# A hybrid decoder layer on one core: outputs stored as high and low parts, the state update added up in PSUM, a one-column mix on ScalarE, and other figures in the kernel's order model

## The chip, the core and the metric

The program runs on one core of one Trainium2 chip. The metric is the device time of one execution in microseconds (us). TensorE (PE in the profile) multiplies; its weight loads are PEld. VectorE is DVE, ScalarE is ACT, GpSimd is POOL, and SyncE (SP) issues nearly all DMAs.

## What is computed

One layer over 2048 tokens of width 1024, all in float32. Cut to what matters here:

```python
h = LN(x) * (1 + scale) + shift
proj = h @ w_in                                  # 1024 x 4232
rw = rw + (rw_prev - rw) * rwkv_mix              # mix with the token before
# group A, RWKV-7, 8 heads x 64, for each token:
S = S * w_t - (S @ kk_t) b_t^T + v_t k_t^T       # S is 64 x 64 per head
y_a = S @ r_t
# group B, 8 heads x 64: causal softmax attention with a running forget bias
y = concat(GN(y_a) + bonus, y_b) * silu(gate)
out = LN(alpha * x + (1 + gate_c) * (y @ w_out))
```

## The kernel before, in words

**Projections.** TensorE multiplies float32 by splitting each operand into a high part (rounded to fp32r) and the rest: three fp32r matmuls of 128 x 512 per 128-row slice, 24 for a tile of 128 columns and 512 tokens. The weight tile is loaded into `wst` (one buffer), copied to the high part in `wsp` by ACT, and POOL subtracts to get the low part (`weights()`; `wsp` has two buffers, `wb`). There are 66 weight tiles of the input projection with 48 matmuls each, and 16 token tiles of the output projection, also with 48, for which the stored outputs `yscr` take the place of the weights.

**Stages.** The 2048 tokens go in two halves of 1024. For each half the recurrence (`rwkv_stream`, tiles named `rw_s`) comes first and then attention (`fox_stream`, tiles `fx_s`, `fx_p`, `fx_v`). Projection matmuls (`ps<-ht,wsp`) are put between the small matmuls of these stages as filler. Output tiles of the first half serve as filler in the second attention stage; the others follow it, half of all with the tiles `end_s`.

**The recurrence.** It works on chunks of 64 tokens. A batch (`rwkv_batch`, 64 of them: two halves, 8 blocks, 4 batches) does two chunks for a pair of heads. X (`xs`) holds solved right sides for keys and values; Z holds score and key matrices. Before, four matmuls of 128 x 128 x 128 in plain float32 make F = X^T Z for keys and values together; DVE adds two matrices to the key half with four instructions, and ACT copies the value half with two. The state tile then holds [S; I] per head (the unit matrix in the other half of its rows), so that one matmul of 128 rows gives the key part times S plus the value part. Per chunk four matmuls follow, two that give the next state and two that give y, and DVE scales the two halves of the state with two instructions. A plain float32 matmul leaves two records in the trace, an fp32r one or a transpose one.

**The finish.** `rwkv_post` and `fox_out` multiply a result of 128 x 512 by its gate and store it (32 stores). `final_x` reads x again for a token tile and normalises it with DVE, POOL, DVE. `final_tile` runs 48 matmuls; `final_evac` adds on DVE, takes mean and variance, and applies four `scalar_tensor_tensor` of 128 x 512 before the stores.

**What sets the order.** The instructions are not scheduled by the compiler: the kernel's `Driver` runs all streams as generators against its own table of costs (`cost`, `on_pe`) and issues next whatever its clock says is ready, by priority. So each engine's queue is fixed when the program is built, and each engine runs its queue strictly in order. A figure in that table changes the order everywhere behind it. `drv.side()` marks work whose end the stream does not wait for.

`hs(h)` picks rows 0 to 63 or 64 to 127, so that the matmuls of two heads use different parts of the array.

Of the kernel before, what the change touches and what calls it, by code (L numbers as in the profile page):

```python
# [17 lines left out]
D = 1024  # L18
TB = 1024
NB = 512  # L20
# [117 lines left out]
class Driver:  # L138
# [31 lines left out]
    def cost(self, e, op, ops, kw):  # L170
# [3 lines left out]
        if "dma_start" in op:  # L174
            return 450.0 if e.name == "sp" else 1000.0
# [35 lines left out]
    def on_pe(self, t, op, ops):  # L211
# [6 lines left out]
        if nr == nc == 4:  # L218
            d = max(stream + (14 if n >= 256 else 3), load + 2)
        else:  # L220
            d = max(stream + (load if nc < 4 else 6), 25.0)
# [113 lines left out]
def hymba_kernel(ctx: ExitStack, tc, x, c, emb_ln_g, emb_ln_b, w_ada, b_ada, w_in, rwkv_mix, w0,  # L335
# [47 lines left out]
    yscr = [dram.tile([D, TB], F32, name=f"yscr{i}") for i in range(2)]  # L383
# [35 lines left out]
    state = const.tile([128, 2, 4, 2, 64], F32, name="state")  # L419
# [156 lines left out]
    def start_consts():  # L576
# [82 lines left out]
        for b in range(2):  # L659
            for p in range(4):  # L660
                dve.tensor_copy(state[64:128, b, p, 0, :], i64[64:128, :])
                dve.tensor_copy(state[0:64, b, p, 1, :], i64[0:64, :])
            yield
# [200 lines left out]
    def weights():  # L864
# [4 lines left out]
        while True:  # L869
# [77 lines left out]
    def shift_mix(b, g, o):  # L947
# [5 lines left out]
        dve.scalar_tensor_tensor(o[:, 0:1], car[:, g:g + 1], par("mix", g), o[:, 0:1],  # L953
                                 op0=OP.mult, op1=OP.add)
# [452 lines left out]
    def rwkv_batch(p, n, c0, bufs, u, qt, yb, dl, st):  # L1407
# [6 lines left out]
        Xh = xs.ap.rearrange("p (i c) -> p i c", c=128)  # L1414
# [17 lines left out]
        bf = b.ap.rearrange("p (i c) -> p i c", c=128)  # L1432
        for h in range(2):
            i = slice(2 * h, 2 * h + 2)
            tt(Fh[hs(h), i, 0:64], bf[hs(h), i, 0:64], kr[hs(h), g, 1], OP.add)
            tt(Fh[hs(h), i, 64:128], bf[hs(h), i, 64:128], i64[hs(h), None, :].to_broadcast([64, 2, 64]), OP.add)
        for h in range(2):
            o = hs(1 - h)
            i = slice(2 * h, 2 * h + 2)
            act.activation(Fh[o, i, :], bf[o, i, :], AF.Copy)  # L1440
# [4 lines left out]
        for ci in range(2):  # L1445
# [4 lines left out]
            for h in range(2):  # L1450
                i = 2 * h + ci
                mm(b.ap[hs(h), 0:64], Fh[:, i, 64:128], cur[:, h, :])
            with drv.side():
                for h in range(2):
                    i = 2 * h + ci
                    mm(yb.ap[hs(h), cc * 64:(cc + 1) * 64], cur[:, h, :], Fh[:, i, 0:64])
# [6 lines left out]
        st["next"] = (n, c0 + 2) if c0 + 2 < 8 else (n + 1, 0)  # L1463

    def rwkv_post(half, p, blk, yb, bonus):
# [29 lines left out]
        g.free()  # L1495
        yield
        sp.dma_start(yscr[half][p * 128:(p + 1) * 128, blk * NB:(blk + 1) * NB], Y.ap)
        Y.free()
        yield
# [35 lines left out]
    def rwkv_stream(half):  # L1535
# [20 lines left out]
        def elems():  # L1556
            for n in range(8):
# [8 lines left out]
                u.amuse = 2  # L1566
                u.done = done
# [285 lines left out]
    def fox_out(half, p, h, qi, nk, pv, o, sums):  # L1853
# [43 lines left out]
        g.free()  # L1897
        yield
        sp.dma_start(yscr[half][512 + p * 128:640 + p * 128, qi * NB:(qi + 1) * NB], o.ap)
        o.free()  # L1900
        normed[0] += 1
        yield
# [71 lines left out]
    def final_x(i):  # L1974
# [13 lines left out]
        yield  # L1988
        tt(xt.ap, xt.ap, fin["eb"].ap, OP.add)
# [115 lines left out]
```

## Time and profile before

| | us |
|---|---|
| median of 3 runs | 1866.49 |
| lowest and highest | 1865.16, 1883.88 |
| the profiled execution's own time | 1866.47 |
| its span, first to last instruction | 1864.7 |
| PE busy | 1784.5 (96%) |
| DVE busy | 1287.4 (69%) |
| ACT, POOL busy | 804.4, 779.3 |

A row of the timeline is: start us, duration us, engine, source line, operation, output tile <- input tiles, shape, xcount, and in brackets the idle time before it and what ended it. All work is issued through one helper, so every row has line L134; the tile names tell the parts apart. For matmuls the shape is rows*columns of the array, then the moving operand. Ends of matmuls are modelled, so rates are read from start to start.

### The profile page before, as it was taken

To read this page: it belongs to the slowest core of one execution; us is meant where nothing else is said; L and a number is where in the kernel's file an instruction comes from. 1 tells how busy PE (TensorE), PEld (TensorE's weight loads), DVE (VectorE), ACT (ScalarE), POOL (GpSimd) and SP (SyncE) were. 2 spreads that over 40 slices of the span, in tenths; PEclk is the share of its full clock that TensorE was granted. 3 is DMA by queue.
4 is the path that set the end of the run, shared out by engine and by line. 5 is a ranking of instruction groups with operands and counts; after the bars stand their busy time and mean duration, and the time that the engine had idled before them with its cause. 6 is when DMAs were issued, how large, how long until landed. Compare 5 with 4: busy or idle time off the path is not lost.

```text
span 1864.7 us, 35565 instructions
## 1 busy us (share of the span) xinstructions
PE 1784.5 (96%) x13609; PEld 1288.3 (69%) x13609; DVE 1287.4 (69%) x3049; ACT 804.4 (43%) x1571; POOL 779.3 (42%) x773
## 2 busy tenths in 40 slices
PE   8999999999999899999999999989899899999995
PEld 6777777767777656677777777767555356666884
DVE  4987685665773768667657675762677584876998
ACT  2454555354444245554554554443244344432000
POOL 1333242422423357743143442424256364566652
PEclk8999999998999999999999999999899899999998
DMA  8252020210122755132021120213422732512433
GB/s 263 72 163 81 30 69 23 80 51 26 53 87 86 226 172 178 58 115 84 19 78 36 41 79 30 75 39 114 131 92 84 244 111 77 191 57 90 153 115 122
DMA packets 172129, 181.60 MB, mean 97 GB/s; under 512 B 12180, under 2 KB 116197, under 8 KB 171960
## 3 DMA queue, kind: packets, MB, share of 16 engines
q1 hardware_dynamic: 171960, 179.33, 30.6%
q8 instruction: 108, 1.77, 0.4%
q14 instruction: 61, 0.50, 0.1%
HBM read 132.10 MB, written 47.13 MB: 96 GB/s over the span
## 4 chain that ended last, share of the span: by engine, by line
PE 55%; DVE 5%; ACT 3%; SPq 3%; DMA 2%; issue 2%; POOL 1%; DVEq 0%; ACTq 0%; POOLq 0%
PE ps L134 55%; SPq L134 3%; ACT rw_s L134 2%; DVE rw_s L134 2%; DMA arena<-vscr 1%; DVE end_s L134 1%; DVE small L134 1%; DVE arena L134 1%; POOL rw_s L134 0%; POOL wsp L134 0%; DMA arena<-in_b_ada_dram 0%; ACT arena L134 0%; DMA yscr<-rw_s 0%; DVE fx_p L134 0%; DMA fx_s<-qscr 0%
## 5 line engine op out<-in xcount | busy, mean ns | idle before, releaser
L134 PE MATMUL ps<-ht,wsp 128*128 128x512 f32 x3840 | 976.4, 400 | 3.4 <-POOL wsp L134 1.3
L134 PEld LDWEIGHTS ps<-ht,wsp 128*128 128x128 f32 x3840 | 701.1, 189 | 163.3 <-issue 15.0
L134 POOL TENSOR_TENSOR wsp<-wst,wsp 128x1024 fp32r<-128x1024 f32 x79 | 192.8, 2440 | 320.2 <-ACT wsp L134 256.2
L134 ACT ACTIVATE rw_s<-ps 64x256 f32<-64x256 f32 (+3 forms) x544 | 215.9, 409 | 200.7 <-PE ps L134 101.0
L134 PE MATMUL ps<-fx_s 67*128 67x512 f32 (+6 forms) x960 | 261.1, 390 | 12.3 <-DMA fx_s<-kscr 4.0
L134 ACT ACTIVATE fx_p<-ps 128x512 f32<-128x512 f32 (+3 forms) x336 | 162.8, 521 | 196.2 <-PE ps L134 175.6
L134 PEld LDWEIGHTS ps<-fx_s 67*128 67x128 f32 (+1 forms) x960 | 165.4, 193 | 118.3 <-issue 47.7
L134 POOL TENSOR_TENSOR fx_p<-fx_p 128x512 f32<-128x512 f32 (+2 forms) x160 | 185.7, 1167 | 140.7 <-PE ps L134 138.3
L134 PE MATMUL ps<-rw_s 32*32 32x32 f32 (+4 forms) x5376 | 227.7, 217 | 17.0 <-DVE rw_s L134 8.0
L134 PEld LDWEIGHTS ps<-rw_s 32*32 32x32 f32 (+3 forms) x5376 | 195.7, 130 | 66.1 <-issue 26.6
L134 DVE TENSOR_TENSOR rw_s<-rw_s 128x24 f32<-128x24 f32 (+11 forms) x544 | 179.8, 336 | 26.0 <-ACT rw_s L134 12.6
L134 DVE TENSOR_REDUCE small<-ps 128x1 f32<-128x512 f32 (+1 forms) x208 | 134.5, 683 | 44.4 <-PE ps L134 43.6
L134 ACT ACTIVATE arena<-ps 128x512 f32<-128x512 f32 (+3 forms) x128 | 74.1, 581 | 191.6 <-PE ps L134 161.7
L134 POOL TENSOR_TENSOR small<-small,nhalf 128x8 f32<-128x8 f32 (+1 forms) x48 | 68.3, 1425 | 211.6 <-DVE small L134 211.5
L134 PE MATMUL ps<-fx_p,fx_v 128*64 128x512 f32 (+3 forms) x640 | 155.9, 556 | 0.0
L134 DVE TENSOR_TENSOR fx_p<-fx_p 128x512 f32<-128x512 f32 (+1 forms) x128 | 111.9, 874 | 51.6 <-POOL fx_p L134 48.9
L134 ACT ACTIVATE wsp<-wst 128x1024 fp32r<-128x1024 f32 x80 | 84.3, 1054 | 134.2 <-PE ps L134 110.1
L134 DVE TENSOR_SCALAR state<-ps,dl 64x64 f32<-64x64 f32 x256 | 72.4, 283 | 64.2 <-PE ps L134 57.2
L134 POOL TENSOR_TENSOR rw_s<-rw_s,arena 128x512 f32<-128x512 f32 x64 | 84.9, 1328 | 69.4 <-ACT arena L134 39.2
L134 DVE TENSOR_TENSOR arena<-ps,arena 128x512 fp32r<-128x512 f32 (+4 forms) x108 | 72.5, 677 | 54.0 <-ACT arena L134 50.3
L134 POOL TENSOR_SCALAR rw_s<-rw_s 64x128 f32<-64x128 f32 x128 | 38.0, 297 | 120.0 <-PE ps L134 109.4
L134 ACT ACTIVATE rw_s<-rw_s 32x256 f32<-32x256 f32 (+2 forms) x112 | 70.0, 653 | 39.4 <-DVE rw_s L134 38.7
(152 smaller groups left out, 1864.9 us busy)
## 6 DMA issues: line engine op xcount, KB each, us to landing
wst<-in_w_in_dram SPq DMA_DIRECT2D x66, 512.0 KB
fx_s<-kscr SPq DMA_DIRECT2D x144, 128.0 KB
fx_s<-qscr SPq DMA_DIRECT2D x96, 128.0 KB
ada_t<-in_w_ada_dram SPq DMA_DIRECT2D x16, 512.0 KB
rw_l<-lowscr SPq DMA_DIRECT2D x32, 256.0 KB
kscr<-arena SPq DMA_DIRECT2D x32, 256.0 KB
qscr<-arena SPq DMA_DIRECT2D x32, 256.0 KB
arena<-in_x_dram SPq DMA_DIRECT2D x16, 512.0 KB
```

Of the source, the lines that this page charges most:

```text
L134: return fn(*args, **kw)
```

## The change

It has six parts.

1. `store_y` splits each output into a high and a low part before it is stored (ACT copy, DVE subtract), and stores both; `yscr` becomes twice as large. The output projection loads both parts straight into `wsp`; its ACT copy and POOL subtract are gone, and it takes a `wsp` buffer before the load and not behind it.
2. In `rwkv_batch`, F holds the key part only (four matmuls of 128 rows and 64 columns). The value part goes straight into the accumulators: four matmuls per batch into y and two per chunk into the next state. The state tile loses its unit matrices, so the state matmuls use 64 rows. DVE adds with two instructions for four and scales with one for two; the two ACT copies are gone.
3. The first column of the token mix moves from DVE to ACT.
4. `final_x` becomes two `scalar_tensor_tensor` on DVE.
5. In the order model a DMA issue on SP to or from over 8 partitions costs 600 and not 450.
6. In the order model a matmul on part of the array costs less when it is narrow.

```diff
-            return 450.0 if e.name == "sp" else 1000.0
+            return (450.0 if list(out.ap)[0][1] <= 8 else 600.0) if e.name == "sp" else 1000.0
...
-            d = max(stream + (load if nc < 4 else 6), 25.0)
+            d = max(stream + 6, load + 5, 52.0)
...
-    state = const.tile([128, 2, 4, 2, 64], F32, name="state")
+    state = const.tile([128, 2, 4, 64], F32, name="state")
...
             if k == "out":
-                sp.dma_start(wst[:, 0], dap(yscr[hf], t0, [[TB, 128], [128 * TB, KT], [1, 128]]))
+                w = yield from wb.get()
+                for i in range(2):
+                    sp.dma_start(w.ap.bitcast(F32)[:, i], dap(yscr[hf], i * D * TB + t0, [[TB, 128], [128 * TB, KT], [1, 128]]))
                 drv.spawn(final_x(p), 0)
+                yield
+                wready.append((it, w))
+                continue
...
-        dve.scalar_tensor_tensor(o[:, 0:1], car[:, g:g + 1], par("mix", g), o[:, 0:1],
-                                 op0=OP.mult, op1=OP.add)
+        act.activation(o[:, 0:1], car[:, g:g + 1], AF.Identity, scale=par("mix", g), bias=o[:, 0:1])
...
-        for i in range(4):
-            o = 2 * (i % 2) + i // 2
-            mm(b.ap[:, o * 128:(o + 1) * 128], Xh[:, i, :], Z[:, i, :])
...
-        for h in range(2):
-            o = hs(1 - h)
-            i = slice(2 * h, 2 * h + 2)
-            act.activation(Fh[o, i, :], bf[o, i, :], AF.Copy)
+        for ci in range(2):
+            for h in range(2):
+                mm(b.ap[hs(h), ci * 128:ci * 128 + 128], X4[:, ci, 192 * h:192 * h + 64], Z[:, 2 * ci + h, :], start=not ci)
+        for ci in range(2):
+            for h in range(2):
+                xv = X4[:, ci, 64 + 64 * h:128 + 64 * h]
+                mm(yb.ap[hs(h), (c0 + ci) * 64:(c0 + ci + 1) * 64], xv, Z[:, 2 * ci + h, 0:64], start=not u.begun[h],
+                   stop=False)
+                u.begun[h] = True
...
-                mm(b.ap[hs(h), 0:64], Fh[:, i, 64:128], cur[:, h, :])
+                mm(b.ap[hs(h), 0:64], Z[:, 2 * ci + h, 64:128], X4[:, ci, 64 + 64 * h:128 + 64 * h], stop=False)
+            for h in range(2):
+                mm(b.ap[hs(h), 0:64], Fh[hs(h), ci, 64:128], cur[hs(h)], start=False)
...
-            ts(nxt[0:64, 0, :], b.ap[0:64, 0:64], dl[0:64, cc:cc + 1], None, OP.mult)
-            ts(nxt[64:128, 1, :], b.ap[64:128, 0:64], dl[64:128, cc:cc + 1], None, OP.mult)
+            ts(nxt, b.ap[:, 0:64], dl[:, cc:cc + 1], None, OP.mult)
...
+    def store_y(half, c0, blk, y, g):
+        act.activation(g.r, y.ap, AF.Copy)
+        yield
+        tt(y.r, y.ap, g.ap, OP.subtract)
+        to = yscr[half]
+        cols = slice(blk * NB, (blk + 1) * NB)
+        sp.dma_start(to[0, c0:c0 + 128, cols], g.ap)
+        g.free()
+        yield
+        sp.dma_start(to[1, c0:c0 + 128, cols], y.ap)
+        y.free()
+        yield
...
-        ts(xt.ap, xt.ap, stats[:, i, 0:1], stats[:, i, 1:2], OP.subtract, OP.mult)
-        yield
-        pool.tensor_tensor(xt.ap, xt.ap, fin["eg"].ap, op=OP.mult)
-        yield
-        tt(xt.ap, xt.ap, fin["eb"].ap, OP.add)
+        dve.scalar_tensor_tensor(xt.ap, xt.ap, stats[:, i, 0:1], fin["eg"].ap, op0=OP.subtract, op1=OP.mult)
+        yield
+        dve.scalar_tensor_tensor(xt.ap, xt.ap, stats[:, i, 1:2], fin["eb"].ap, op0=OP.mult, op1=OP.add)
```

The order moves on every engine. In the lists below the size is that of the output (partitions x columns) and xcount counts matmuls, not records. TensorE in the recurrence of the first half, before, two batches with two chunks between: `rw_s 128x128` is F = X^T Z, `state,rw_s` gives the next state and `rw_s,state` gives y.

```order
L134 MATMUL ps<-ht,wsp 128x512 x9
L134 MATMUL ps<-state,rw_s 64x64 x2
L134 MATMUL ps<-rw_s,state 64x64 x2
L134 MATMUL ps<-rw_s 128x128 x4
L134 MATMUL ps<-state,rw_s 64x64 x2
L134 MATMUL ps<-rw_s,state 64x64 x2
L134 MATMUL ps<-ht,wsp 128x512 x9
```

The same place in the changed kernel: `rw_s 64x128` is F, `rw_s 64x64 x4` the value part of y, `rw_s 64x64 x2` the value part of the next state.

```order
L134 MATMUL ps<-ht,wsp 128x512 x18
L134 MATMUL ps<-rw_s 64x128 x4
L134 MATMUL ps<-rw_s 64x64 x4
L134 MATMUL ps<-rw_s 64x128 x4
L134 MATMUL ps<-rw_s 64x64 x4
L134 MATMUL ps<-ht,wsp 128x512 x3
L134 MATMUL ps<-rw_s 64x64 x2
L134 MATMUL ps<-state,rw_s 64x64 x2
L134 MATMUL ps<-rw_s,state 64x64 x2
L134 MATMUL ps<-ht,wsp 128x512 x6
```

F moved from the full array to runs of half-width matmuls, and each chunk has a run of two ahead of its four. TensorE's list has 1927 rows (stretches of equal instructions) before and 2130 now. Of the 64 groups for F, 14 stand alone between matmuls of the full array, and 18 run straight on into a chunk's first two; the others touch some other small run.

TensorE at the start of the second attention stage, before, up to the transposes of the values (`ident,arena`), which wait for a load:

```order
L134 MATMUL ps<-ht,wsp 128x512 x3
L134 MATMUL ps<-fx_s 128x128
L134 MATMUL ps<-ht,wsp 128x512 x3
L134 MATMUL ps<-fx_s 128x256
L134 MATMUL ps<-ht,wsp 128x512 x3
L134 MATMUL ps<-fx_s 128x384
L134 MATMUL ps<-ident,arena 128x128 x4
L134 MATMUL ps<-fx_s 128x512 x10
```

In the changed kernel, from the same score matmul of 384 columns on:

```order
L134 MATMUL ps<-fx_s 128x384
L134 MATMUL ps<-fx_s 128x512 x2
L134 MATMUL ps<-ht,wsp 128x512 x3
L134 MATMUL ps<-fx_s 128x512
L134 MATMUL ps<-ht,wsp 128x512 x3
L134 MATMUL ps<-fx_s 128x512 x3
L134 MATMUL ps<-ident,small 4x128
L134 MATMUL ps<-fx_s 128x512 x2
L134 MATMUL ps<-ht,wsp 128x512 x3
L134 MATMUL ps<-fx_s 128x512
L134 MATMUL ps<-ident,arena 128x128 x4
```

Eighteen matmuls of 512 columns (nine `fx_s`, nine `ht,wsp`) now stand between that score matmul and the transposes that wait.

VectorE at the end of the program, before:

```order
L134 SCALAR_TENSOR_TENSOR end_s<-end_s,small,arena 128x512 x2
L134 TENSOR_SCALAR small<-small 128x1
L134 TENSOR_TENSOR small<-small 128x1
L134 SCALAR_TENSOR_TENSOR end_s<-end_s,small,arena 128x512 x2
L134 TENSOR_TENSOR small<-small 128x1 x2
L134 SCALAR_TENSOR_TENSOR end_s<-end_s,small,arena 128x512 x3
L134 TENSOR_SCALAR small<-small 128x1
L134 SCALAR_TENSOR_TENSOR end_s<-end_s,small,arena 128x512
L134 TENSOR_TENSOR small<-small 128x1
L134 SCALAR_TENSOR_TENSOR end_s<-end_s,small,arena 128x512 x7
```

and in the changed kernel, from the last addition of a matmul's result on:

```order
L134 TENSOR_TENSOR end_s<-ps,end_s 128x512
L134 BN_STATS small<-end_s 128x6
L134 BN_AGGR small<-small 128x2
L134 TENSOR_SCALAR small<-small 128x1
L134 TENSOR_TENSOR small<-small 128x1 x2
L134 TENSOR_SCALAR small<-small 128x1
L134 TENSOR_TENSOR small<-small 128x1
L134 SCALAR_TENSOR_TENSOR end_s<-end_s,small,arena 128x512 x4
```

Before, 22 of these SCALAR_TENSOR_TENSOR stand behind the last addition of a matmul's result, four to a token tile; now the four of the last tile do.

## Rows read from the trace of the kernel before

**Rows 1.** The page: busy us, share and count by engine.
```profile
PE 1784.5 (96%) x13609; PEld 1288.3 (69%) x13609; DVE 1287.4 (69%) x3049; ACT 804.4 (43%) x1571; POOL 779.3 (42%) x773
```

**Rows 2.** The waits of PE: us in total, times, longest; the main ones.
```profile
PE ps L134 <- ACT rw_s L134: 10.8, 23, 1.3
PE ps L134 <- DMA arena<-vscr: 10.2, 6, 6.1
PE ps L134 <- DVE rw_s L134: 8.0, 6, 2.9
...
PE ps L134 <- DMA fx_s<-kscr: 4.0, 3, 2.8
```

**Rows 3.** Timeline of PE in the recurrence, shapes of the array.
```profile
406.49 1.16 PE L134 MATMUL ps<-rw_s 64*128 64x128 f32 x16
407.58 0.72 PE L134 MATMUL ps<-rw_l,bones 128*128 128x512 f32 x2
408.15 1.05 PE L134 MATMUL ps<-rw_s 128*128 128x128 f32 x8
409.04 0.71 PE L134 MATMUL ps<-ident,rw_s 128*128 128x128 f32 x5
409.68 0.45 PE L134 MATMUL ps<-rw_s 64*64 64x64 f32 x8
410.05 0.33 PE L134 MATMUL ps<-ident,rw_s 128*128 128x128 f32 x1
...
423.82 2.34 PE L134 MATMUL ps<-ht,wsp 128*128 128x512 f32 x9
426.08 0.34 PE L134 MATMUL ps<-state,rw_s 128*64 128x64 f32 x4
...
426.47 1.16 PE L134 MATMUL ps<-rw_s 128*128 128x128 f32 x8
```

**Rows 4.** Groups of DVE and ACT instructions: count, busy us, mean ns.
```profile
L134 DVE TENSOR_SCALAR state<-ps,dl 64x64 f32<-64x64 f32 x256 | 72.4, 283 | 64.2 <-PE ps L134 57.2 <-ACT rw_s L134 1.1
L134 ACT ACTIVATE rw_s<-ps 64x256 f32<-64x256 f32 x256 | 95.4, 377 | 138.4 <-DVE rw_s L134 92.1 <-PE ps L134 42.8
```

**Rows 5.** Stretches: us, busy by engine, granted clock, DMA share, GB/s.
```profile
432.00:446.00 14.00, 14.00 (x207) 10.42 (x207) 3.33 (x12) 6.79 (x17) 2.85 (x5) 0.51 0.13 37
616.00:620.00 4.00, 4.00 (x14) 3.07 (x13) 1.45 (x5) 0.23 (x1) 0.00 (x0) 0.58 0.70 202
1330.00:1340.00 10.00, 8.32 (x22) 5.12 (x23) 4.27 (x10) 4.26 (x8) 3.22 (x2) 0.50 0.45 139
```

**Rows 6.** Timeline of PE, the end of the program.
```profile
1784.63 59.32 PE L134 MATMUL ps<-ht,wsp 128*128 128x512 f32 x261
```

**Rows 7.** The chain that ended last, from 1800 us: start us, us, what.
```profile
1843.99 0.69 DVE end_s L134
...
1857.06 3.98 DVE end_s L134 x6
1861.04 0.66 DVEq L2101
```

**Rows 8.** Timeline of the end: DVE and POOL.
```profile
1750.83 3.38 POOL L134 TENSOR_TENSOR arena<-arena 128x1024 f32<-128x1024 f32 x1
...
1751.87 2.88 DVE L134 TENSOR_SCALAR arena<-arena,stats 128x1024 f32<-128x1024 f32 x1
...
1783.22 0.80 DVE L134 TENSOR_SCALAR end_s<-end_s,stats 128x1024 f32<-128x1024 f32 x1
...
1845.52 1.27 DVE L134 BATCH_NORM_STATS2 small<-end_s 128x6 f32<-128x512 f32 x2
...
1849.92 1.00 POOL L134 TENSOR_TENSOR small<-small,nhalf 128x1 f32<-128x1 f32 x1 [3.68 <-DVE small L134]
```

**Rows 9.** Timelines of SP and ACT: a weight load and the copy behind it.
```profile
625.53 0.41 SPq L134 DMA_DIRECT2D wst<-in_w_in_dram  x1
...
631.83 1.06 ACT L134 ACTIVATE wsp<-wst 128x1024 fp32r<-128x1024 f32 x1 [7.91 <-DMA wst<-in_w_in_dram]
```

More of the change, by code (lines that the diff above doesn't have):

```diff
@@ L381, in hymba_kernel @@
     wb = Banks(drv, wspr, [0, 1])
-    yscr = [dram.tile([D, TB], F32, name=f"yscr{i}") for i in range(2)]
+    yscr = [dram.tile([2, D, TB], F32, name=f"yscr{i}") for i in range(2)]
     cscr = [dram.tile([3, 8, TB], F32, name=f"cscr{i}") for i in range(2)]
@@ L658, in start_consts @@
         ts(maskmm[:, 64:128], tmp.ap[:, 64:128], 0.0, None, OP.is_ge)
[L659 to L662, printed above, removed]
-            yield
         for i in range(8):
@@ L1413, in rwkv_batch @@
         X4 = xs.ap.rearrange("p (c i) -> p c i", i=256)
-        Xh = xs.ap.rearrange("p (i c) -> p i c", c=128)
         Fh = q.ap.rearrange("p (i c) -> p i c", c=128)
@@ L1427, in rwkv_batch @@
         b = yield from pb.get()
-        for i in range(4):
-            o = 2 * (i % 2) + i // 2
-            mm(b.ap[:, o * 128:(o + 1) * 128], Xh[:, i, :], Z[:, i, :])
-        yield
-        bf = b.ap.rearrange("p (i c) -> p i c", c=128)
-        for h in range(2):
-            i = slice(2 * h, 2 * h + 2)
-            tt(Fh[hs(h), i, 0:64], bf[hs(h), i, 0:64], kr[hs(h), g, 1], OP.add)
-            tt(Fh[hs(h), i, 64:128], bf[hs(h), i, 64:128], i64[hs(h), None, :].to_broadcast([64, 2, 64]), OP.add)
-        for h in range(2):
-            o = hs(1 - h)
-            i = slice(2 * h, 2 * h + 2)
-            act.activation(Fh[o, i, :], bf[o, i, :], AF.Copy)
+        for ci in range(2):
[7 more added lines that the diff above has]
+                u.begun[h] = True
+        yield
+        bf = b.ap[:, 0:256].rearrange("p (i c) -> p i c", c=128)
+        tt(Fh[:, 0:2, 64:128], bf[:, :, 64:128], i64[:, None, :].to_broadcast([128, 2, 64]), OP.add)
+        tt(Fh[:, 0:2, 0:64], bf[:, :, 0:64], kr[:, g, 1], OP.add)
         b.free()
@@ L1450, in rwkv_batch @@
             for h in range(2):
-                i = 2 * h + ci
-                mm(b.ap[hs(h), 0:64], Fh[:, i, 64:128], cur[:, h, :])
+                mm(b.ap[hs(h), 0:64], Z[:, 2 * ci + h, 64:128], X4[:, ci, 64 + 64 * h:128 + 64 * h], stop=False)
+            for h in range(2):
+                mm(b.ap[hs(h), 0:64], Fh[hs(h), ci, 64:128], cur[hs(h)], start=False)
             with drv.side():
                 for h in range(2):
-                    i = 2 * h + ci
-                    mm(yb.ap[hs(h), cc * 64:(cc + 1) * 64], cur[:, h, :], Fh[:, i, 0:64])
+                    mm(yb.ap[hs(h), cc * 64:(cc + 1) * 64], cur[hs(h)], Fh[hs(h), ci, 0:64], start=False)
             yield
-            ts(nxt[0:64, 0, :], b.ap[0:64, 0:64], dl[0:64, cc:cc + 1], None, OP.mult)
-            ts(nxt[64:128, 1, :], b.ap[64:128, 0:64], dl[64:128, cc:cc + 1], None, OP.mult)
+            ts(nxt, b.ap[:, 0:64], dl[:, cc:cc + 1], None, OP.mult)
             b.free()
@@ L1494, in rwkv_post @@
         tt(Y.ap, Y.ap, g.ap, OP.mult, pool)
-        g.free()
         yield
-        sp.dma_start(yscr[half][p * 128:(p + 1) * 128, blk * NB:(blk + 1) * NB], Y.ap)
-        Y.free()
-        yield
+        yield from store_y(half, p * 128, blk, Y, g)
         ystored[half] += 1
@@ L1566, in elems @@
                 u.amuse = 2
+                u.begun = [False, False]
                 u.done = done
@@ L1896, in fox_out @@
         tt(o.ap, o.ap, g.ap, OP.mult, pool)
-        g.free()
         yield
-        sp.dma_start(yscr[half][512 + p * 128:640 + p * 128, qi * NB:(qi + 1) * NB], o.ap)
-        o.free()
+        yield from store_y(half, 512 + p * 128, qi, o, g)
         normed[0] += 1
-        yield
         ystored[half] += 1
```

1 line of the change is left out of this document (removed).

## Prediction

> **What bounds the kernel now.** The page comes first: PE is busy for 1784.5 of 1864.7 us, and no other engine for over 69% [rows 1]. A busy PE is not a full one, so I read next how fast its matmuls follow each other, from start to start [rows 3, 6], and then what PE waited for [rows 2]. At the end of the program 261 matmuls of 128x512 take 59.32 us, 0.227 each [rows 6], with hardly a gap; between the small matmuls of the recurrence nine of the same cost 2.26 us, 0.25 each [rows 3]. So nearly every microsecond of PE work that the change adds or removes moves the end, and work of DVE, ACT, POOL and SP counts only where PE waits for it, or behind PE's last matmul. That last part is a stage of its own: the last result is added at 1843.99, and the chain goes on in DVE alone until 1861.04, with the end at 1864.7 [rows 7].
>
> **PE in the recurrence: about +30 us.** Rates [rows 3]:
> - the full array: eight records of 128 columns from 408.15 to 409.04, 0.89 us;
> - half the array (128*64): eight records of 64 columns (four for the state, four for y) from 426.08 to 426.47, 0.39;
> - half the array (64*128): sixteen records of 128 columns from 406.49 to 407.58, 1.09;
> - a quarter (64*64): eight records of 64 columns from 409.68 to 410.05, 0.37.
>
> Two halves run side by side, or they could not be this fast. The second and third rows separate a run's fixed price from its columns: 0.70 us more for 1536 more columns is 0.456 ns a column, and 0.39 less 512 of them leaves 0.157 us for each run. A batch before: 0.89 for F and two runs of 0.39, 1.67 us. Now F (eight records of 128 columns) and the value part of y (eight of 64) make one run of 1536 columns: 0.157 + 0.700 = 0.857. Per chunk the value part of the state is a run of 256 columns, 0.157 + 0.117 = 0.274, and then state and y at 64*64 cost 0.37. Together 0.857 + 2 x 0.644 = 2.145, which is 0.475 more; times 64 batches 30.4 us. The order says how many of these runs join others: 14 groups for F stand alone, and each cuts a stretch of projection in two. The price of that is what nine projection matmuls lose between small runs, 2.26 less 9 x 0.227, 0.2 us: +2.8. Eighteen join the next chunk's run and save its fixed price: -2.8. So +30.
>
> Bounds: if none of the new runs paid the fixed price (64 and 128 of them, 30 us) the sum would be 0, and if all 64 stood alone, +43. A gain is excluded by the columns: what F loses on the full array comes back as columns of the value parts. The nearest row is the fixed 0.157, which stands for runs of each shape, so I keep 30. No row shows a run of 128*64 followed at once by one of 64*64, as each of the 128 chunks now has.
>
> The Trainium skill, TensorEngine Tiling (Array Packing), section Tiling Modes, Key Properties, speaks against the change here: another tiling mode, not merely another tile, drains TensorE first. By that rule each of the 128 new pairs pays and the sum stays; without it the sum would be 20 us less. The same page (Restrictions and Gotchas, PSUM Pressure) says that different row tiles can't access one PSUM bank at the same time, which would put the two heads' new 64*64 matmuls one behind the other; what that would give is among the rivals.
>
> **What hides on other engines.** DVE scaled the state with 256 instructions of 283 ns and ACT copied F with half of 256 instructions of 377 ns [rows 4]; half of the first (36 us) and all of the second (48 us) go, and half of DVE's four additions per batch. None of this is on the path except where PE waits for them: ACT 10.8 and DVE 8.0 us in `rw_s` [rows 2]. I take 7 of these 18.8 back, bounds 0 and 14. The split in `store_y` adds 32 ACT copies and 32 DVE subtractions of 128x512 and 32 more DMA issues, and takes away 16 POOL subtractions and 16 ACT copies of twice that width (1.06 us for such a copy [rows 9]). The mix column adds 52 short instructions to ACT. All this lies beside PE, which has other matmuls to run; if the cover fails, the first to wait are the projection's evacuations, and then the 7 us above are lost. The new wait, on a `wsp` buffer at the load, stands in SP's queue: behind it stand the next x load and two output stores. PE does one token tile in 48 x 0.227 = 10.9 us. A load of 512 KB took at most 6.3 us, from its issue at 625.53 to the copy it released at 631.83 in a crowded stretch [rows 9]; both parts take 12.6 then. At its worst that is 1.7 us a tile, 14 us over the eight tiles of the end; at its best, where the two fit into 10.9, nothing. In the end stage fewer other transfers run, so I take nothing and keep the 14.
>
> **The end: -11 us.** Before, 22 `scalar_tensor_tensor` stand behind the last addition; six of them take 3.98 us [rows 7], 0.66 each, 14.6 us in all. Why DVE is so late is in the rows as well: a `tensor_scalar` of 128x1024 takes 0.80 us alone and 2.88 beside a POOL instruction of 3.38 [rows 8]. Now POOL has neither the subtraction nor the product of `final_x` there. DVE's work for one tile is eight passes over 512 columns at 0.66 (two additions, two statistics, four scalings), 5.3 us, two of 1024 at twice that, 2.6, and some 1 us of small ones: 8.9 us against PE's 10.9, so no queue builds up and only the last tile stands behind PE. Its last half: addition 0.69, statistics 1.27/2, POOL's power 1.00, small ones about 0.8, four scalings 2.64: 5.8 us. With the 3.7 us from DVE's end to the program's end that is 9.5, where now 1864.7 - 1843.99 = 20.7 stand: -11.2. Bounds: -14 if the small ones hide, and 0 if DVE is as late as now.
>
> **The order model: -16 us.** PE waited 10.2 us for `arena<-vscr` and 4.0 for `fx_s<-kscr` [rows 2]. The longest of them, 6.1 us, is at the start of the second attention stage. Eighteen matmuls of 512 columns now stand ahead of the waiting transposes there, about 4 us of work. Behind two of these waits the granted clock was 0.50 for 10 us and 0.58 for 4 [rows 5], nearly the lower level of 1.2 GHz for 2.4, so another 5.0 and 1.7 us were lost. Together 20.9; I take 16, bounds -21 and +8 (new waits of half that size, since a new order can also put consumers too early).
>
> **The sum.** +30 - 7 - 11 - 16 = -4. The profiled execution took 1866.47, 1.8 more than its span, and that is the median of the runs to 0.02. So 1862 us. About 1% (18.7 us) is what a measurement of this kernel can tell from no change: 1847.8 to 1885.2.
>
> **Rivals.**
> - *Cheap shape changes (faster).* If a run of 64*64 may follow one of 128*64 without the fixed price, 128 x 0.157 = 20 us go: 1842. For it: both use half of the array's width, and each run writes other columns of the array than the one before it, in part. Against it: every run in the rows pays. Fuller success of the order model would add up to 5 more. Chance 0.32, together with better orders in places that I didn't read.
> - *The clock (slower).* In the recurrence the granted clock fell to 0.51 from 432 to 446 [rows 5], right after a stretch of small runs with waits: 14 us x 0.49 = 6.9 us lost. The change puts more small runs there. Four more such falls over the 16 blocks cost 28: 1890. It decides from four on; three leave 1883. For it: more runs, less of the array in use. Against it: the waits of ACT and DVE shrink. Chance 0.14.
> - *One bank, one row tile (slower).* By the rule above, state and y at 64*64 would take eight records one at a time, 0.0555 each (half of 0.111), 0.44 + 0.157 = 0.60 for 0.37: 128 x 0.23 = 29 us, 1891. Against it: the 64*64 matmuls of the kernel now (scores times values) read different row halves, write to one bank and take 0.37 for eight [rows 3]. Chance 0.03.
> - *Late loads at the end.* 14 us of it give 1876, still within 1%; it's in the forecast's range.
>
> **How the numbers follow.** The forecast's case, within 1%, has 0.50, the faster rival 0.32, the slower ones 0.17, and I give the last 0.01 to slower. The forecast's own range is 1850 to 1880. To hold 8 in 10 it reaches into both sides: down to 1834 (the faster rival with the order model's full 21 and the end's 14) and up to 1889.
>
> **What would show it.** PE records up by 1024 (16 more per batch); runs of four value records before each chunk, with about 0.27 us from start to start; PE's busy time up in the two recurrence stages by some 15 us each; 9 to 10 us between the last matmul and the end; the wait for `arena<-vscr` under 4 us; the same few stretches at half clock. The forecast is wrong if the state runs follow at 0.15 us or below, if PE waits for `wsp` loads in the end stage, or if half-clock stretches multiply in the recurrence.

## The result, and the profile after

The changed kernel takes **1842.5 us** (median of 4 runs, 1837.5 to 1843.0), against 1865.8 for the kernel before in the same comparison: a ratio of 0.9863 [0.9827, 0.9899]. The forecast was 1862 with a range of 1834 to 1889. So the time lies in the range, but it came out in the faster case (0.32) and not in the likeliest, within 1% (0.50). The profiled execution is the fastest of the four (1837.49 us, span 1835.5). It stands 29.2 us below the one before, where the medians differ by 23.

The page of the changed kernel: busy time by engine [rows 1], and the granted clock in 40 slices.

```profile
PE 1791.4 (98%) x14633; PEld 1292.8 (70%) x14633; DVE 1216.2 (66%) x2757; ACT 778.0 (42%) x1511; POOL 694.6 (38%) x741
...
PEclk8999999999999999899999999999999999999999
```

PE has 1024 records more, as forecast, and only 7 us more busy time; busy time includes half clock, so this says little yet. PE's waits [rows 2], for ACT, DVE and the two loads:

```profile
PE ps L134 <- ACT rw_s L134: 5.2, 14, 0.7
...
PE ps L134 <- DMA arena<-vscr: 2.7, 2, 2.5
...
PE ps L134 <- DMA fx_s<-kscr: 1.4, 1, 1.4
...
PE ps L134 <- DVE rw_s L134: 0.3, 2, 0.2
```

All four waits that the prediction spoke of shrank: 18.8 to 5.5 us for ACT and DVE, 14.2 to 4.1 for the two loads. At the start of the second attention stage, where the longest load wait stood (6.1 us), PE now waits for the two parts of a weight tile (timeline of PE):

```profile
1323.00 1.22 PE L134 MATMUL ps<-ht,wsp 128*128 128x512 f32 x2 [2.36 <-ACT wsp L134]
1325.42 0.79 PE L134 MATMUL ps<-ht,wsp 128*128 128x512 f32 x1 [1.20 <-POOL wsp L134]
```

The timeline of PE in the first recurrence [rows 3]:

```profile
405.58 0.89 PE L134 MATMUL ps<-rw_s 128*64 128x128 f32 x16
406.40 0.96 PE L134 MATMUL ps<-ht,wsp 128*128 128x512 f32 x3
...
409.50 0.34 PE L134 MATMUL ps<-rw_s 128*64 128x64 f32 x4
409.77 0.33 PE L134 MATMUL ps<-state,rw_s 64*64 64x64 f32 x4
409.93 0.28 PE L134 MATMUL ps<-rw_s,state 64*64 64x64 f32 x4
410.14 0.97 PE L134 MATMUL ps<-ht,wsp 128*128 128x512 f32 x3
```

From start to start: F with the value part of y takes 0.82 us (forecast 0.857), a value run 0.27 (0.274), state and y 0.37 (0.37). A value run has 256 columns, 0.117 us at 0.456 ns each, so 0.153 us of fixed price is paid right ahead of the 64*64 run. The Trainium skill, TensorEngine Tiling (Array Packing), section Tiling Modes, Key Properties, says that another tiling mode drains TensorE. The rows agree in that a price is paid there; that a drain is what costs it, no run shows.

The end [rows 6, 7]: the last stretch of matmuls, and the last row of the chain of waits.

```profile
1769.65 56.60 PE L134 MATMUL ps<-ht,wsp 128*128 128x512 f32 x249
```

```profile
1831.69 0.75 DVE end_s L134
```

PE ends at 1826.3, 9.2 us before the end of the span (forecast 9.5, before 20.7). The two recurrence stages, one row each (us, busy time by engine, granted clock, DMA):

```profile
127.70:558.80 431.10, 426.54 (x5042) 325.44 (x5042) 263.77 (x719) 210.36 (x417) 156.89 (x162) 1.00 0.20 60
837.60:1275.70 438.10, 434.64 (x5094) 334.20 (x5094) 261.58 (x727) 214.06 (x422) 158.47 (x163) 1.00 0.19 58
```

Length less PE busy is idle time: 4.6 and 3.5 us, 8.0 together, where the same stages idled 24.5 us before; and the clock is full throughout. One sign of the forecast did not come: PE's busy time in these stages was to rise by some 15 us each, and it fell, from 450.6 to 426.5 and from 444.0 to 434.6. The order put 174 fewer projection matmuls there (39 us at 0.227 each), and 8.5 us of half clock are gone; so busy time tells about the work only together with these two.

**One reckoning for all kernels.** The span is a sum of four: PE's idle time up to its last matmul; half-clock time (half of what PE is busy while the trace shows the lower level of its clock, 1.2 GHz); the tail behind PE's last matmul; and the rest, which is PE's work at full clock. Before: 59.4 + 24.4 + 20.7 + 1760.2. After: 34.8 + 16.2 + 9.2 + 1775.3. So work rose by 15.1, and idle time, half clock and tail gave back 24.6, 8.2 and 11.5. The table has this for every kernel below; "filler" counts the projection matmuls (`ps<-ht,wsp`) that the order put into the two recurrence stages, of 3840 under that name in the whole program.

| kernel | median us | ratio [95%] | work | idle + half clock | of these in the recurrence | filler | tail |
|---|---|---|---|---|---|---|---|
| before | 1865.2 to 1866.5 | | 1760.2 | 83.8 | 24.5 + 8.5 | 2133 | 20.7 |
| after | 1842.5 | 0.9863 [0.9827, 0.9899] | 1775.3 | 51.0 | 8.0 + 0 | 1959 | 9.2 |
| e1_state | 1888.7 | 1.0116 [1.0088, 1.0143] | 1777.3 | 91.9 | 22.9 + 23.9 | 1923 | 21.6 |
| e2_finish | 1877.1 | 1.0069 [1.0042, 1.0095] | 1757.7 | 103.1 | 26.6 + 13.6 | 2277 | 9.2 |
| e3_model | 1879.4 | 1.0068 [1.0042, 1.0094] | 1769.0 | 100.6 | 14.4 + 0 | 2343 | 11.5 |
| e4_all_but_model | 1874.5 | 1.0050 [1.0028, 1.0072] | 1772.9 | 102.4 | 22.7 + 4.9 | 2004 | 9.2 |
| e5_all_but_state | 1871.5 | 1.0032 [1.0021, 1.0043] | 1761.9 | 98.0 | 9.4 + 0 | 2379 | 9.7 |
| e6_no_issue | 1852.8 | 0.9934 [0.9912, 0.9956] | 1778.2 | 62.4 | 9.8 + 0 | 2052 | 9.2 |
| e7_no_small | 1864.9 | 0.9992 [0.9970, 1.0014] | 1771.8 | 78.5 | 21.5 + 0 | 2004 | 9.2 |
| e8_one_run | 1827.2 | 0.9796 [0.9763, 0.9829] | 1759.9 | 54.5 | 15.6 + 0 | 2169 | 9.7 |
| l1_580 | 1843.0 | 0.9869 [0.9832, 0.9906] | 1774.8 | 58.8 | 6.5 + 0 | 1950 | 9.5 |
| g1_gap_long | 1863.5 | 0.9975 [0.9949, 1.0001] | 1775.8 | 74.7 | 22.5 + 10.2 | 1959 | 9.2 |
| g2_gap_short | 1839.7 | 0.9860 [0.9838, 0.9882] | 1778.3 | 49.8 | 10.1 + 0 | 1959 | 9.2 |
| g3_modelled | 1844.4 | 0.9885 [0.9862, 0.9909] | 1777.9 | 54.0 | 9.6 + 0 | 2181 | 9.2 |

The split is of one profiled execution each, the median of all runs; the two can differ: e4's profile is the slowest of its ten executions (1886 us), e2's the second fastest of ten (1872).

### The profile page after: what moved, and what is told of

Same layout as the page of the kernel before. It is cut to its first block, busy times and chain, and to the rows that moved or that the text cites. A ratio compares the mean times of both kernels' runs of the same rounds, so it can differ in the third digit from the quotient of the medians.

```text
span 1835.5 us, 37107 instructions
## 1 busy us (share of the span) xinstructions
PE 1791.4 (98%) x14633; PEld 1292.8 (70%) x14633; DVE 1216.2 (66%) x2757; ACT 778.0 (42%) x1511; POOL 694.6 (38%) x741
## 4 chain that ended last, share of the span: by engine, by line
PE 52%; DVE 2%; SPq 1%; issue 1%; ACT 1%; DMA 1%; POOL 0%; POOLq 0%; DVEq 0%
PE ps L134 52%; SPq L134 1%; ACT rw_s L134 1%; DVE small L134 0%; DVE rw_s L134 0%; DVE arena L134 0%; DMA arena<-vscr 0%; DMA wst<-in_w_in_dram 0%; DVE end_s L134 0%; POOL wsp L134 0%; DVE ht L134 0%; DVE fx_p L134 0%; DVE ps L134 0%; ACT fx_p L134 0%; ACT arena L134 0%
## 5 line engine op out<-in xcount | busy, mean ns | idle before, releaser
L134 PEld LDWEIGHTS ps<-ht,wsp 128*128 128x128 f32 x3840 | 699.1, 188 | 169.1 <-issue 13.6
L134 PEld LDWEIGHTS ps<-rw_s 32*32 32x32 f32 (+4 forms) x6400 | 202.0, 125 | 91.4 <-issue 54.7
L134 PE MATMUL ps<-fx_s 67*128 67x512 f32 (+3 forms) x960 | 258.5, 387 | 4.0 <-DMA fx_s<-kscr 1.4
L134 PE MATMUL ps<-rw_s 32*32 32x32 f32 (+6 forms) x6400 | 252.3, 219 | 7.2 <-ACT rw_s L134 5.2
L134 POOL TENSOR_TENSOR wsp<-wst,wsp 128x1024 fp32r<-128x1024 f32 x63 | 152.4, 2419 | 270.6 <-ACT wsp L134 270.6
L134 ACT ACTIVATE rw_s<-ps 32x256 f32<-32x256 f32 (+3 forms) x416 | 168.6, 418 | 176.0 <-PE ps L134 150.2
L134 DVE TENSOR_TENSOR rw_s<-rw_s 128x24 f32<-128x24 f32 (+11 forms) x544 | 173.5, 325 | 22.7 <-ACT rw_s L134 10.9
L134 ACT ACTIVATE arena<-ps,pc 128x512 f32<-128x512 f32 x70 | 49.3, 715 | 81.9 <-PE ps L134 77.5
L134 DVE TENSOR_SCALAR state<-ps,dl 128x64 f32<-128x64 f32 x128 | 36.0, 281 | 70.9 <-PE ps L134 68.6
L134 DVE CUSTOM_DVE_ANT_0 ps<-ps,mneg 128x128 f32<-128x128 f32 (+3 forms) x128 | 61.5, 507 | 32.3 <-PE ps L134 31.4
```

The source lines that it names most:

```text
L134: return fn(*args, **kw)
```

## Experiments

**First series: the parts alone.** Three theories: A, work (the added runs count in full); C, relief (part 2's shorter chain pays for them); and B, a draw of the order (the time moves either way, by waits in places that the part doesn't touch).

*e1_state*: part 2 alone.

```diff
-                mm(b.ap[hs(h), 0:64], Fh[:, i, 64:128], cur[:, h, :])
+                mm(b.ap[hs(h), 0:64], Z[:, 2 * ci + h, 64:128], X4[:, ci, 64 + 64 * h:128 + 64 * h], stop=False)
...
+                mm(b.ap[hs(h), 0:64], Fh[hs(h), ci, 64:128], cur[hs(h)], start=False)
```

> Part 2 of the change alone (F for the keys only, value parts added in PSUM, no unit matrices in the state); the rest as before. Theory A, work: the added runs of small matmuls, 64 x 0.475 = 30 us, count in full and only 7 us of ACT's and DVE's waits come back: about 1889 us, ratio 1.012. Theory C, relief: the shorter chain through ACT and DVE lets PE's waits and the half-clock stretches in the two recurrence stages go, and pays for the runs and more: 1850 to 1866, with the idle time of PE in these stages at half or less of before. Theory B, a draw of the order: the time lies anywhere within 15 us of 1866, with new waits or half-clock stretches in stages that part 2 doesn't touch.

Measured: 1888.7, the number of theory A. But its parts are others: work rose by 17, not 30; idle time in the recurrence hardly fell (24.5 to 22.9); half clock in it rose from 8.5 to 23.9. The two waits that the prediction named did shrink, from 18.8 to 7.2 us, but another one took their place, for the state that DVE scales (0.2 us before; waits of PE in this kernel):

```profile
PE ps L134 <- DVE state L134: 11.0, 8, 2.0
```

Theory C falls: part 2 alone moves the waits, and hardly shortens them.

*e2_finish*: parts 1 and 4; of each, what it adds at the core.

```diff
+                w = yield from wb.get()
+                for i in range(2):
+                    sp.dma_start(w.ap.bitcast(F32)[:, i], dap(yscr[hf], i * D * TB + t0, [[TB, 128], [128 * TB, KT], [1, 128]]))
...
+        dve.scalar_tensor_tensor(xt.ap, xt.ap, stats[:, i, 1:2], fin["eb"].ap, op0=OP.mult, op1=OP.add)
```

> Parts 1 and 4 alone (outputs split where they are made and loaded straight into wsp, final_x as two steps on DVE). A and C: the end, from the last matmul to the end of the program, falls from 20.7 to 9 to 10 us and nothing else changes: about 1855 us, ratio 0.994. B: the same at the end, but the rest moves by up to 15 us either way.

Measured: 1877.1, 12 slower. The tail is 9.2, as all theories said. The rest got longer, which only theory B allows. Idle time and half clock rose by 19.3 us in the profiled execution: 13.6 of them in the first attention stage, where 23.9 us at half clock begin within a wait of 5.67 us, 7.2 in the recurrence, and only 1.5 in the second attention stage, though the longest wait of all stands there (timeline of PE and stretches of this kernel, the first attention stage and then the second):

```profile
649.76 1.09 PE L134 MATMUL ps<-ident,arena 128*128 128x128 f32 x4 [5.67 <-ACT wsp L134]
...
1384.68 3.14 PE L134 MATMUL ps<-arena,ct 128*32 128x512 f32 x8 [10.42 <-DMA arena<-in_w_ada_dram]
```

```profile
648.10:672.00 23.90, 20.93 (x57) 11.70 (x57) 15.25 (x48) 8.43 (x17) 6.72 (x9) 0.50 0.58 202
1378.60:1388.80 10.20, 4.12 (x11) 1.30 (x12) 0.42 (x3) 0.00 (x0) 0.00 (x0) 0.50 0.98 293
```

The DMA engines are 98% busy in the last of these stretches. A part that is right by its own count can lose it all where the order moves.

*e3_model*: parts 5 and 6.

```diff
-            return 450.0 if e.name == "sp" else 1000.0
+            return (450.0 if list(out.ap)[0][1] <= 8 else 600.0) if e.name == "sp" else 1000.0
...
-            d = max(stream + (load if nc < 4 else 6), 25.0)
+            d = max(stream + 6, load + 5, 52.0)
```

> Parts 5 and 6 alone (the two figures of the order model), no instruction added or taken away. A, where the order model has the gain that the added runs hide: DMA waits and the half clock behind them go, 16 us, about 1850, ratio 0.991. C, where part 2 makes the gain: within 5 us of before. B: anywhere within 15 us, waits of other tiles in place of those that went.

Measured: 1879.4, 14 slower, a miss for A and C and within B's 15. In the recurrence the figures do what was hoped: idle time 24.5 to 14.4, half clock 8.5 to 0 (stretches of this kernel, then the second attention stage):

```profile
128.30:586.10 457.80, 450.63 (x4686) 349.22 (x4686) 300.27 (x864) 228.71 (x466) 161.66 (x165) 1.00 0.21 63
827.60:1314.70 487.10, 479.92 (x4818) 371.78 (x4818) 309.37 (x871) 235.38 (x476) 169.83 (x168) 1.00 0.22 65
1333.10:1750.90 417.80, 393.46 (x1639) 220.80 (x1639) 316.77 (x561) 151.15 (x299) 228.41 (x210) 0.93 0.33 107
```

Then it is lost behind: 24.3 us idle (417.80 less 393.46) at a mean clock of 0.93 in the second attention stage, and waits at the start of the end stage. Two of the gaps (timeline of PE):

```profile
1358.98 0.80 PE L134 MATMUL ps<-fx_s 67*128 67x512 f32 x1 [6.58 <-ACT mrow L134]
...
1778.41 1.22 PE L134 MATMUL ps<-ht,wsp 128*128 128x512 f32 x2 [8.75 <-ACT wsp L134]
```

The recurrence took 2343 projection matmuls as filler, 210 more than before. What it took is missing later: 450 stand in the end stage, where there were 633.

*e4_all_but_model*: parts 1 to 4, the two figures as in the `-` lines of the diff just shown.

> The whole change without its two figures of the order model (parts 1 to 4). A: +30 - 7 - 11, about 1878 us, ratio 1.006; the waits for arena<-vscr and fx_s<-kscr are as before, 14 us. C: the recurrence is as short as with the whole change, 1840 to 1852. B: within 15 us of 1855, and not the sum of what parts 2 and 1 with 4 give alone.

Measured: 1874.5, near A's 1878, and the waits for the two loads are as before (13.4 us), as A said. In the recurrence the idle time is 22.7 us, as with the old figures everywhere, against 8.0 with the new ones. PE waits 7.4 us for `state` here too, and 0.3 in the changed kernel. So the figures, not part 2, take the recurrence's waits away; and they gain 32 us beside parts 1 to 4 (1874.5 to 1842.5) but lose 14 alone.

**Second series: which figure, and what the added runs cost.**

*e6_no_issue* and *e7_no_small*: the changed kernel with one of the two figures put back.

```diff
-            return (450.0 if list(out.ap)[0][1] <= 8 else 600.0) if e.name == "sp" else 1000.0
+            return 450.0 if e.name == "sp" else 1000.0
```

> The whole change without part 5 (a DMA issue costs 450 in the order model, as before). Measure used: length of the two recurrence stages less 0.227 us for each projection matmul in them; 435 us before, 424 with the whole change, 444 without both figures, 413 with both figures alone. Theory F, the small-tile figure makes the recurrence's gain: 424 plus or minus 5, and the whole time differs from the changed kernel's 1842 only by PE's gaps and half-clock stretches in the attention stages, up to 30 us more. Theory G, the issue figure makes it: about 444 in the recurrence, 1862 or more.

```diff
-            d = max(stream + 6, load + 5, 52.0)
+            d = max(stream + (load if nc < 4 else 6), 25.0)
```

> The whole change without part 6 (matmuls on part of the array cost as before in the order model). F: the recurrence stages less their projection go back to 444 us plus or minus 5, by more gaps of PE and more cuts of the projection, so about 1862, and more where the attention stages draw gaps. G: 424, about 1842.

Measured: 1852.8 and 1864.9. Theory F holds. The recurrence stages less 0.227 us for each projection matmul are 427 in e6 and 439 in e7. Their rows in e7, with 10.7 and 10.8 us idle where the changed kernel has 4.6 and 3.5:

```profile
124.60:571.40 446.80, 436.09 (x5093) 334.63 (x5093) 261.00 (x721) 211.09 (x420) 159.86 (x163) 1.00 0.19 60
840.10:1287.00 446.90, 436.10 (x5089) 335.16 (x5088) 264.76 (x732) 213.42 (x422) 159.69 (x163) 1.00 0.18 57
```

The small-tile figure is worth 22 us in this kernel (1864.9 to 1842.5), the issue figure 10 (1852.8 to 1842.5). Beside parts 1 to 4 the two simply add up: starting from e4, with neither, the small-tile figure alone gives 21.7 (e6) and the issue figure alone 9.6 (e7). They also do different things. Without the issue figure the waits for the two loads are back (waits of PE in e6), 16.5 us where the changed kernel has 4.1:

```profile
PE ps L134 <- DMA arena<-vscr: 11.4, 5, 6.8
...
PE ps L134 <- DMA fx_s<-kscr: 5.1, 6, 1.9
```

Without the small-tile figure the waits of the recurrence are back (21.5 us idle there), and the load waits stay low (5.0).

*e8_one_run*: value parts of the next state for both chunks in F's run, in one bank `bv`.

```diff
+        bv = yield from pb.get()
+        for ci in range(2):
+            for h in range(2):
+                mm(bv.ap[hs(h), ci * 64:ci * 64 + 64], Z[:, 2 * ci + h, 64:128], X4[:, ci, 64 + 64 * h:128 + 64 * h],
+                   start=not ci, stop=False)
...
             for h in range(2):
-                mm(b.ap[hs(h), 0:64], Z[:, 2 * ci + h, 64:128], X4[:, ci, 64 + 64 * h:128 + 64 * h], stop=False)
-            for h in range(2):
-                mm(b.ap[hs(h), 0:64], Fh[hs(h), ci, 64:128], cur[hs(h)], start=False)
+                mm(vb[hs(h)], Fh[hs(h), ci, 64:128], cur[hs(h)], start=False)
```

> The whole change, and the value part of the next state is added up for both chunks in one bank in the same run as F and the value part of y, so that the 128 runs of four value records ahead of a chunk's state matmuls are gone; same matmuls, same columns. If each of those runs costs its fixed price: 128 x 0.157 = 20 us less PE work, 1822, less what the order draws (up to 10 either way). If what the added runs cost was given back by fewer cuts of the projection, as many cuts come back and the time stays within 8 us of 1842.

Measured: 1827.2, 15 below the changed kernel and **faster than both**. Work fell by 15.4 (1775.3 to 1759.9) with the same matmuls and columns, so the price of a run is real: 15.4 us for 128 runs is 0.12 each, of 0.157 expected. This is a net figure, since work also moves with the order alone (by 6.5 us among the other kernels with part 2); in the recurrence stages by themselves the small runs take 19 us less from start to start, 0.15 each. A chunk in this kernel (timeline of PE), with no value run ahead of the state's:

```profile
423.68 0.96 PE L134 MATMUL ps<-ht,wsp 128*128 128x512 f32 x3
424.57 0.33 PE L134 MATMUL ps<-state,rw_s 64*64 64x64 f32 x4
424.73 0.28 PE L134 MATMUL ps<-rw_s,state 64*64 64x64 f32 x4
424.95 0.96 PE L134 MATMUL ps<-ht,wsp 128*128 128x512 f32 x3
```

*l1_580*: the changed kernel with another issue figure.

```diff
-            return (450.0 if list(out.ap)[0][1] <= 8 else 600.0) if e.name == "sp" else 1000.0
+            return (450.0 if list(out.ap)[0][1] <= 8 else 580.0) if e.name == "sp" else 1000.0
```

> The whole change with 580 for 600 as the issue figure; every instruction is the same, and the order differs only from the first attention stage on. Theory D, draw: outside the first recurrence stage the gaps of PE over 1.2 us and the half-clock stretches behind them fall elsewhere and in another number; the time lies 5 to 25 us above 1842, and all of it is idle time of PE and half clock. Theory S, the figure is right: 580 is nearer to 600 than to 450, and the time is within 3 us of 1842.

Measured: 1843.0, as theory S says. A draw that scatters by 5 to 25 us at every small move isn't what this kernel shows; one such figure doesn't exclude it for others.

**Third series: what a gap costs.** Most half-clock stretches so far stood behind a gap of PE of 1 us or more; is it the gap?

*g1_gap_long*, *g2_gap_short* (`range(2)`), *g3_modelled* (the same four issued through the order model):

```diff
+        if n % 2 and c0 == 2:
+            for _ in range(4):
+                nc.vector.tensor_tensor(gapt[:], i64[:, None, :].to_broadcast([128, 8, 64]),
+                                        i64[:, None, :].to_broadcast([128, 8, 64]), op=OP.add)
```

> The changed kernel with an artificial delay: in 8 of the 64 recurrence batches VectorE does four more additions of 128x512 (about 0.69 us each, 2.7 together) right before the additions that make F, and the order model isn't told, so TensorE's queue is the same instruction for instruction. Theory H, a gap costs twice: TensorE stands idle 1.5 to 2.7 us at each place, and each such gap is followed by a half-clock stretch of 3.4 to 13.7 us, as after the gaps seen so far; 12 to 22 us of idle time and 14 to 55 us of half clock, 1868 to 1919 us. Rival I, the half clock has another cause and only happens to stand near gaps: the idle time alone, at most 22 us, no half-clock stretch in the recurrence, at most 1864.

> The same with two additions in place of four, 1.4 us at 8 places; TensorE's queue is again the same. H: gaps under 1.3 us were mostly followed by no half clock in the runs so far, so the price is the idle time alone, up to 11 us: 1842 to 1853. I: the same. If half-clock stretches stand behind these too, the length of the gap isn't what decides: 1856 and more.

> The same four additions at the same 8 places, and the order model knows of them, so it puts other matmuls in their time. The order changes from the first of them on. H: no gaps, no half clock in the recurrence; what remains is the order's own difference, 1836 to 1854. If VectorE's extra 22 us itself costs TensorE time, through later evacuations, it is as long as with the unmodelled delay, above 1860.

Measured: 1863.5, 1839.7 and 1844.4. With TensorE's queue unchanged, g1 has 14.5 us more idle time in the recurrence, and four half-clock stretches there where the changed kernel has none (10.2 us lost). Of its six gaps over 1.3 us in these stages, from 1.4 to 2.6 us long, four were followed by one. One of them (timeline of PE, then the stretch ahead and the one behind):

```profile
942.04 0.34 PE L134 MATMUL ps<-rw_s 128*64 128x64 f32 x4
943.78 0.33 PE L134 MATMUL ps<-state,rw_s 64*64 64x64 f32 x4 [1.41 <-DVE state L134]
```

```profile
930.00:942.00 12.00, 12.00 (x232) 9.31 (x216) 3.62 (x10) 8.54 (x20) 4.62 (x4) 1.00 0.05 9
943.98:950.80 6.82, 6.82 (x51) 4.93 (x49) 1.74 (x7) 0.76 (x2) 1.22 (x3) 0.50 0.01 2
```

So H holds in kind: the gap brings the half clock, and dense work without one, small runs and projection mixed, didn't here (1.00 over the 12 us ahead). The length of a gap alone doesn't decide it: the one of 1.41 us was followed by a stretch, the ones of 1.48 and 2.07 us in the first half weren't. Its price was put too high: 10 us of half clock in place of 14 to 55, and the total of 1863.5 lies in I's bounds. The short delay gives no gap over 0.9 us in the recurrence and costs nothing that can be measured (1839.7, a little under H's 1842 to 1853); the modelled one is filled (one gap of 1.49 us is left, such as e6 and e8 have without any delay), so VectorE's extra work costs nothing clear of noise where the order knows of it.

*e5_all_but_state*: the changed kernel with F and the state as before (the `-` lines of e1's diff for its `+` lines).

> The whole change without part 2 (F in full and the state with its unit matrices, as before). By the prediction's terms part 2 costs 30 - 7 = 23 us: 1819. By the recurrence stages of the runs so far (less 0.227 us for each projection matmul: 435 before, 413 with both figures alone, 424 with the whole change) it costs 11 beside the new figures: 413 plus or minus 4 in these stages, and 1831 in all if the attention stages draw what they do in the changed kernel; gaps there can add 20. If part 2 is what made the gain, 1855 or more with 435 in the recurrence.

Measured: 1871.5, 29 slower than with part 2, a miss in the total. The recurrence is 411, as expected from the earlier runs, and work is 13 us less than with part 2. All of that and more is lost behind: 75 us of idle time and half clock outside the recurrence and the start, where the changed kernel has 27. Its worst places (timeline of PE, then the stretches):

```profile
1349.72 1.08 PE L134 MATMUL ps<-ident,arena 128*128 128x128 f32 x4 [6.05 <-DMA arena<-vscr]
...
1378.54 1.08 PE L134 MATMUL ps<-ident,arena 128*128 128x128 f32 x4 [7.61 <-DMA arena<-vscr]
...
1769.17 1.22 PE L134 MATMUL ps<-ht,wsp 128*128 128x512 f32 x2 [10.85 <-DMA wsp<-yscr]
```

```profile
1348.80:1386.30 37.50, 25.93 (x65) 17.14 (x65) 24.91 (x59) 4.24 (x10) 0.00 (x0) 0.50 0.61 190
1761.80:1775.40 13.60, 5.86 (x13) 4.18 (x14) 6.03 (x10) 0.00 (x0) 0.04 (x1) 0.50 0.90 267
```

The recurrence took 2379 projection matmuls, 420 more than in the changed kernel, and the end stage kept 459 of 660; there PE waits 10.85 us for the last outputs to go to memory and come back. In e3, which kept 450, the 8.75 us shown above are the same wait (its copy waits for the load of `yscr`); in the changed kernel this time lies beside output tiles of the first half, and PE is never idle in the end stage. In the four kernels without part 2 the losses (idle time and half clock) outside the recurrence and the start grow with the filler that it took: 35 us at 2133, 51 at 2277, 71 at 2343, 75 at 2379. With part 2 it takes 1923 to 2181, and they are 23 to 43, save in e4 (63 at 2004). That filler is the cause is the reading that fits; no run changed the filler alone, so it is argued and not shown.

## Why the prediction came out as it did

- **PE in the recurrence, +30.** Right in mechanism, twice too big. The prices of the runs came out within 0.04 us, and e8 shows that they are paid. But work rose by 15 against before, by 17 in e1 against before, by 15 in e4 against e2 and by 13 against e5. The step that failed is the trips, the price of each cut that small runs make in a stretch of projection: the prediction let it cancel against the runs that join others (+2.8 - 2.8). From e5 to the changed kernel, which differ in part 2 alone, the small runs take 25 us more (from start to start, waits taken out), near the forecast's 27.6 without trips; and the projection in these stages goes from 285 stretches to 223, and what it takes above 0.227 us a matmul from 51 to 41 us. A stretch is no longer than it was (8.3 and 8.8 matmuls): there are fewer cuts because 420 fewer projection matmuls are put in. Why part 2 makes the order put in fewer is not shown.
- **Other engines' waits, -7.** Undersized: 13.3 of the 18.8 us went, and all idle time and half clock in these stages fell from 33.0 to 8.0. The reason given (less work on ACT and DVE) isn't enough: e1 has that work gone, and there the two waits fall too, but one for `state` comes in their place and PE idles 22.9 us. The small-tile figure, for which the prediction had no term, did it (21.5 to 26.6 us idle in the five kernels with the old one, 6.5 to 15.6 with the new one, g1 aside).
- **The end, -11.** Right: -11.5, and 9.2 to 9.7 us are left in every kernel with parts 1 and 4. These two alone bring it (e2: 9.2); but the figures alone also leave only 11.5 (e3), so it isn't their gain only.
- **The order model, -16.** The forecast stood for the two load waits and the half clock behind them. They did fall (14.2 to 4.1), and it is the issue figure that does it, worth 10 us. But other waits came: idle time and half clock outside the recurrence and the start fell from 35 to 27 us, 8 where 16 stood. At the very place of the longest wait, 6.1 us, PE now waits 2.4 and 1.2 us for a weight tile. The step that failed is that the term held only waits of loads seen before, and priced the figures without the other parts: the small-tile figure is worth another 22 us. From e7 to the changed kernel, 13.5 us of idle time go in the recurrence and 16 of idle time and half clock outside it and the start, for 3.5 more of work. Alone the two figures are 14 us slower, beside parts 1 to 4 they are 32 faster.
- **The sum.** By the medians, parts 1 to 4 cost 9 us (e4 against before), where the prediction had +30 - 7 - 11 = +12, and the figures gave 32, where it had 16. That the first came out close is luck: work rose by 13 in e4 and not by 30, and idle time and half clock rose by 19 in its profile where -7 stood. In the profiled pair idle time and half clock fell by 32.8 where -7 and -16 stood, 9.8 more; work rose by 15.1, 14.9 less; the tail fell by 0.5 more; 1862.5 - 9.8 - 14.9 - 0.5 is 1837.3, and 1837.5 was measured. Both large misses had the same sign, which is why the likeliest case was wrong by a little over 1%; the range held because it was wide enough for both.
- **Rivals.** Cheap shape changes: not seen, each pair pays. That this rival's 1842 is the measured time is luck; of it, only the clause on "better orders" is what happened. The clock: it did bite in e1 (23.9 us in the recurrence), but not in the changed kernel, where the recurrence has neither a gap over 0.8 us nor half clock. One bank, one row tile: state and y take 0.37, not 0.60, though the two heads' matmuls write one bank from different row tiles; the Trainium skill's sentence that different row tiles can't access the same PSUM bank at the same time (TensorEngine Tiling (Array Packing), Restrictions and Gotchas, PSUM Pressure) isn't borne out by these rows. Late loads: the end stage runs 249 matmuls in 56.60 us, 0.227 each, so none.

## What to carry to other kernels

Split a span into work, idle time, half clock and tail, and compare kernels by these: here work was the same within 12 us among kernels of equal content, while idle time and half clock ranged from 50 to 103 us. In a kernel whose order comes from a model, price the parts of a change together: the five subsets e1 to e5 were each slower than before, by 0.3 to 1.2%, e7 was equal, and of the sets that were run only those with part 2 and the small-tile figure both in were faster. Part 2 itself costs 23 us alone (e1), together with part 3 it gains 3 beside parts 1 and 4 with the old figures (e4 against e2), and it gains 29 beside all the rest (the changed kernel against e5). Moving matmuls into a run that exists already is worth its fixed price (0.12 to 0.15 us here) each time.

## What the hardware showed that was not expected

Gaps of PE of 1.4 to 2.6 us in the middle of dense work were followed by 3.4 to 6.8 us at 1.2 GHz in four of six cases (g1). A gap at the start of the second attention stage was followed by much more: 3.18 us of it by 37.5 us, with hardly a wait inside (e4; the 37.5 us in e5 have further waits in them). The wait and the stretch:

```profile
1341.99 1.09 PE L134 MATMUL ps<-ident,arena 128*128 128x128 f32 x4 [3.18 <-DMA arena<-vscr]
```

```profile
1341.60:1379.10 37.50, 37.11 (x90) 19.46 (x90) 19.44 (x42) 11.32 (x22) 12.25 (x12) 0.50 0.19 58
```

So a wait of PE can cost far more than its length. A long gap isn't the only thing that brings the lower clock, though: at the same place in e8 a stretch of 17 us at half clock begins after 13 us with no gap over 0.3 us (two stretches of that kernel). What brought it there stays open.

```profile
1310.00:1323.20 13.20, 12.41 (x48) 8.32 (x46) 12.64 (x33) 0.00 (x0) 0.00 (x0) 1.00 0.58 175
1323.30:1340.20 16.90, 12.33 (x24) 6.65 (x24) 12.10 (x27) 3.80 (x8) 2.37 (x1) 0.50 0.71 245
```

The spread between executions of one kernel goes with the clock as well: the ten of e2 run from 1871 us at a mean clock of 0.977 to 1895 at 0.961, the ten of g1 from 1852 at 0.987 to 1869 at 0.979.
